# Layer 0's FFN: modulation sums by VectorE in pieces loaded ahead, a second F-tile in plain products, and other places for the way out's first operands

## The chip, the cores and the metric

The kernel runs on one core of a Trainium2 chip. TensorE (PE) multiplies matrices, VectorE (DVE), ScalarE (ACT) and GpSimd (POOL) work on tiles element by element, and SyncE (SP) issues nearly all DMAs. Each engine takes its instructions in order; semaphores tie them together. The metric is device time in microseconds. The kernel before takes 1764.14 us, the median of three runs (1763.58 to 1764.52).

## The reference

Two layers over 512 latent tokens (x) and 256 context tokens (ctx) of width 1024. Each layer has an attention and an FFN, and each of these is framed by a modulation: six vectors a layer, for each of the two kinds of token, from a conditioning vector.

```python
for l in range(DEPTH):
    mx = s_c @ mod_w[l] + mod_b[l]        # latent tokens
    mc = s_cc @ mod_w[l] + mod_b[l]       # context tokens
    shx1, scx1, gx1, shx2, scx2, gx2 = split(mx, 6)
    ...
    x = x + gx1 * attention(...)
    x = x + gx2 * swiglu(rms(x, norm_ffn_w[l]) * (1 + scx2) + shx2, ffn_w_in[l], ffn_w_out[l])
    ...  # the same for ctx in layer 0; the last layer needs x alone behind its attention

def swiglu(h, w_in, w_out):
    gate, up = split(h @ w_in, 2)         # 1024 -> 2 x 2816
    return (silu(gate) * up) @ w_out      # 2816 -> 1024
```

The parts of a modulation are numbered 0 to 5 in that order: (1, 5) is the FFN gate of layer 1. A part has 1024 columns and is worked out in four chunks of 256 columns. For the latent tokens and the context tokens there are two sums over the same weights, two "streams"; where only the latent tokens need it, one.

## The kernel before

Everything is float32. A product is made of three matmuls in TensorE's faster float type: each operand is split into a high part (a cast, by ACT) and a low part (a subtraction, by DVE or POOL), and high x high, low x high and high x low are summed. `wbh` and `wbl` are the two parts of a weight block, `hT` of the normed tokens, `hTt` of the difference T2.

Layer 0's FFN has two stages. **Gate and up** goes over 22 F-tiles of 128 hidden columns. F-tile 0 is computed in plain products, from four weight quarters (G1, U1 over the first half of the 1024 inputs, G2, U2 over the second) times two halves of the tokens. Every other tile takes the seven products P1 to P7 of a Strassen-Winograd scheme: their left operands are blocks of the tokens or differences of them (B.., T1 to T4), their right ones quarters of the weights or differences of those (S1 to S4, `ws`). Each product is 12 matmuls of 128x384 (L862). ACT copies partial results out of PSUM (`s`, L867), DVE adds them up (`cg` L885, `c` L890) and forms the hidden values (`hid` L895, L896), which are stored to memory as one tile of 768 tokens (`hidm`) and read back later. `block_order` is the order of the products, written out by hand; PE follows the program's order in this stage. The weight operands are made six ahead in a ring.

**The way out** (`way_out0`) multiplies the hidden values by the second weight in two passes of three token tiles, six PSUM banks each. For each F-tile it loads `hr` (hidden values) and `wdr` (weights), splits both (ACT L924 and L339, DVE L925 and L340), and runs 18 matmuls (L960 to L962) of 128x512.

In these two stages the modulations of what comes next are worked out beside the matmuls. Four chunks of (0, 5) are multiplied by PE (`mod_steps`, L181 and L190). The others go through `mods_by_pool`: a chunk's weights are loaded in two pieces (`modw`, 512 KB), ACT multiplies four blocks by their scalars (L216), POOL adds them (L217 to L222), PE sums over the partitions (the row, L228) and turns the row into columns (L237), and DVE adds a bias (`modc`, L249). `hooks`, a table by F-tile, says when a group of chunks begins, and when its row and its columns are issued; a group in the gate and up stage takes 2.5 F-tiles. `gates_out` turns a gate's columns back into rows (`gps`, L261, and DVE's copy `grow`, L263) and keeps them in memory.

All engines but PE are ordered by a scheduler that goes by dependences and priorities; pools and rings set when a buffer is free.

Of the kernel before, what the change touches and what calls it, by code (L numbers as in the profile page):

```python
# [18 lines left out]
P = 128  # L19
# [43 lines left out]
def backbone(es: ExitStack, tc: tile.TileContext, x, c, ctx, c_ctx, mod_w, mod_b, norm_mix_w, norm_ffn_w,  # L63
# [133 lines left out]
    def mods_by_pool(chunks, pool, bank=None):  # L197

        width = 256
        def bank_tile(name, shape):  # L200
            return tr_tile(name, shape) if bank is None else p_1.tile(shape, F32, name=name, tag=bank)

        all_accs = []
        for l, part, n, streams in chunks:
            c0 = part * D + n * width
            accs = [pool.tile([P, width], F32, name="ma", tag="ma", bufs=4) for _ in range(streams)]
            for pc in range(2):
                w = pool.tile([P, 4, width], F32, name="modw", tag="mw", bufs=2)
                nc.sync.dma_start(
                    w, mod_w[l, pc * 4 * P:(pc + 1) * 4 * P, c0:c0 + width].rearrange("(j p) n -> p j n", p=P))  # L210
                for i, acc in reversed(list(enumerate(accs))):

                    pr = pool.tile([P, 4, width], F32, name="modp", tag="mp", bufs=1) if i else w
                    for k in range(4):
                        kk = 8 * i + 4 * pc + k
                        nc.scalar.activation(pr[:, k], w[:, k], AF.Copy, scale=cols[:, kk:kk + 1])  # L216
                    nc.gpsimd.tensor_add(pr[:, 0:2], pr[:, 0:2], pr[:, 2:4])  # L217
                    if pc == 0:
                        nc.gpsimd.tensor_add(acc, pr[:, 0], pr[:, 1])
                    else:  # L220
                        nc.gpsimd.tensor_add(pr[:, 0], pr[:, 0], pr[:, 1])
                        nc.gpsimd.tensor_add(acc, acc, pr[:, 0])  # L222
            all_accs.extend(accs)
        def finish():
            ps = bank_tile("modrow", [P, width])

            for j, acc in enumerate(all_accs):
                nc.tensor.matmul(ps[32 * j:32 * j + 32, :], cst[:, C_ONE:C_ONE + 32], acc, start=True, stop=True,  # L228
                                 tile_position=(0, 32 * j))
            m = len(all_accs)  # L230

            r = all_accs[0]
# [7 lines left out]
            for l, part, n, streams in chunks:  # L240
# [3 lines left out]
        return finish()  # L244
# [523 lines left out]
    def block_order(first_half, second_half, hooks=None):  # L768
# [3 lines left out]
        for f in range(2, NF):  # L772
            order += [(f, "P1"), (f, "P5"), (f - 1, "P4")] + (hooks or {}).get(f - 0.5, []) + [(f, p) for p in (("P6", "P2", "P3", "P7") if f < NF - 1 else ("P6", "P2", "P7", "P3"))]
            order += (hooks or {}).get(f, [])
        return order + [(NF - 1, "P4")]

# [11 lines left out]
    def gate_up_blocks(l, N, H, order, first_raw, next_raw, ring, ahead, early, tmp, deep, hid, singles, z, after, done=None):  # L788
# [10 lines left out]
        loaded = 0  # L799

# [28 lines left out]
        def operand(n):  # L829
# [7 lines left out]
            if n:  # L837
                f, name = need[n - 1]
                hi, lo = ops[need[n - 1]]
                (nc.gpsimd if name == "G2" else nc.vector).tensor_sub(lo, raw[need[n - 1]], f32(hi))  # L840
                if name == "U2":
                    load(f + 2)
# [7 lines left out]
        def product(f, p):  # L850
# [14 lines left out]
            def copied(tag):  # L865
                c = tmps[f, tag] = tmp.tile([P, N], F32, name=tag, tag=tag, bufs=deep)
                nc.scalar.copy(c, ps)  # L867
# [23 lines left out]
            elif p == "P4":  # L891
                if N <= 256:
                    nc.vector.tensor_mul(hid(f), gates(), bank(f, 0)[:, :2 * N])
                else:
                    nc.vector.tensor_mul(hid(f)[:, :N], gates()[:, :N], ps)  # L895
                    nc.vector.tensor_mul(hid(f)[:, N:], gates()[:, N:], tmps[f, "c2"])  # L896
# [3 lines left out]
            elif p[:2] == "U2":  # L900
                nc.vector.tensor_mul(hid(f)[:, th * N:(th + 1) * N], tmps[f, "sg"], ps)
# [314 lines left out]
    def differences():  # L1216
        t1 = wide.rearrange("p (k c) -> p k c", c=half)
        (h11, l11), (b12, b22) = (f32(z) for z in H["B11"]), rh
        with tc.high_priority(300):
            for _ in norms[NT - 1]:  # L1220
                pass
# [313 lines left out]
```

## Time and profile before

| | before |
|---|---|
| runs, median (lowest to highest) | 1764.14 us (1763.58 to 1764.52) |
| profiled execution | 1765.05 us |
| its span | 1763.3 us |
| mean granted TensorE clock | 0.983 |
| gate and up of layer 0 | 431.5 to 791.8 us |
| way out of layer 0 | 791.8 to about 987 us |
| DMA over the span | 194.67 MB, mean 110 GB/s |

The span is the profiled program from its first to its last instruction; the device time around it is 1.75 us longer. A row of a timeline has the start, the length, the engine and the line, what was written from what, and in brackets how long the engine sat idle before it and what released it. Matmul rows overlap: from start to start is what one costs.

### The profile page before, as it was taken

The numbers are of one execution on the slowest core, as the hardware profiler recorded it, in microseconds if no ns is written. First come the engines' busy times: TensorE is split into PE (matmuls) and PEld (weight loads), VectorE is DVE, ScalarE is ACT, GpSimd is POOL, SyncE is SP. The second block draws the span as 40 slices with busy tenths as digits, with TensorE's granted clock in tenths as the row PEclk, the third lists the DMA queues.
The fourth block names the chain that finished last, engine by engine and source line by source line (L and its number), as shares of the span: only waits on it lengthen the run. The fifth ranks groups of instructions, "written<-read, shape, count | busy, mean of one in ns | idle before, by whom it ended". The sixth has DMA issues, their size and how long they took to land. (4 is left out here: it accounts for less than half of the span.)

```text
span 1763.3 us, 28606 instructions
## 1 busy us (share of the span) xinstructions
PE 1671.1 (95%) x10410; PEld 1481.1 (84%) x10410; DVE 1087.6 (62%) x1848; ACT 980.9 (56%) x2123; POOL 784.1 (44%) x928
## 2 busy tenths in 40 slices
PE   6999999999899999899899989999998989999999
PEld 4887777677899999897688889899986889999887
DVE  4775555434856665665565547667666498887533
ACT  5555555554447676666554546666665555555321
POOL 2774654733216676645510366666654332222000
PEclk9999999999999999999999999999999989999999
DMA  9111322402345444558665412111104233332432
GB/s 322 43 53 60 105 89 72 144 24 60 117 153 162 147 146 149 175 162 282 203 189 171 144 37 61 37 37 41 44 22 132 66 89 103 109 102 61 132 96 72
DMA packets 214799, 194.67 MB, mean 110 GB/s; under 512 B 19648, under 2 KB 196608, under 8 KB 214656
## 3 DMA queue, kind: packets, MB, share of 16 engines
q1 hardware_dynamic: 214304, 192.62, 35.3%
q8 instruction: 82, 1.34, 0.3%
q14 instruction: 61, 0.50, 0.1%
q10 hardware_dynamic: 352, 0.21, 0.0%
HBM read 179.91 MB, written 12.87 MB: 109 GB/s over the span
## 5 line engine op out<-in xcount | busy, mean ns | idle before, releaser
L835 ACT CAST wbh<-wr 128x512 fp32r<-128x512 f32 x171 | 105.3, 619 | 91.0 <-PE p L862 57.4
L862 PE MATMUL p<-hT,wbh 128*128 128x256 f32 (+1 forms) x696 | 145.7, 303 | 0.0
L840 POOL TENSOR_TENSOR wbl<-wr,wbh 128x512 fp32r<-128x512 f32 x43 | 58.2, 1353 | 189.8 <-ACT wbh L835 175.4
L840 DVE TENSOR_TENSOR wbl<-wr,wbh 128x512 fp32r<-128x512 f32 x128 | 115.3, 905 | 43.1 <-ACT wbh L835 39.5
L435 PE MATMUL inps<-wih,hT 128*128 128x384 f32 x384 | 133.3, 347 | 3.9 <-ACT qkv L642 3.1
L437 PE MATMUL inps<-wih,hT 128*128 128x384 f32 x384 | 131.1, 341 | 0.0
L436 PE MATMUL inps<-wil,hT 128*128 128x384 f32 x384 | 129.9, 338 | 0.0
L862 PE MATMUL p<-t,wbh 128*128 128x384 f32 (+1 forms) x504 | 118.4, 321 | 3.1 <-ACT s L867 3.0
L216 ACT ACTIVATE modw<-modw,cols 128x256 f32<-128x256 f32 x192 | 83.6, 499 | 64.8 <-DMA modw<-in_mod_w_dram 64.7
L862 PE MATMUL p<-hTt,wbh 128*128 128x256 f32 (+1 forms) x504 | 109.0, 308 | 9.4 <-DVE hTt L925 6.1
L862 PEld LDWEIGHTS p<-hT,wbh 128*128 128x128 f32 x696 | 114.4, 194 | 3.0 <-issue 2.5
L835 ACT CAST wbh<-ws 128x512 fp32r<-128x512 f32 x126 | 73.3, 582 | 63.2 <-PE p L862 39.1
L862 PE MATMUL p<-hT,wbl 128*128 128x256 f32 (+1 forms) x348 | 104.8, 301 | 1.9 <-DVE wbl L840 1.9
L340 POOL TENSOR_TENSOR wil<-wir,wih 128x768 fp32r<-128x768 f32 x42 | 79.2, 1888 | 61.2 <-ACT wih L339 60.4
L960 PE MATMUL dps<-wdh,hdh 128*128 128x512 f32 x252 | 101.5, 403 | 4.5 <-ACT hdh L924 3.1
L961 PE MATMUL dps<-wdl,hdh 128*128 128x512 f32 x252 | 100.8, 400 | 3.2 <-DVE wdl L340 3.2
L217 POOL TENSOR_TENSOR modw<-modw 128x512 f32<-128x512 f32 x48 | 65.6, 1367 | 80.1 <-ACT modw L216 75.5
L962 PE MATMUL dps<-wdh,hdl 128*128 128x512 f32 x252 | 100.4, 398 | 0.0
L340 DVE TENSOR_TENSOR wdl<-wdr,wdh 128x1024 fp32r<-128x1024 f32 x62 | 82.5, 1333 | 22.4 <-ACT wdh L339 22.1
L565 POOL TENSOR_SCALAR Pt<-Pt,rc 128x256 f32<-128x256 f32 (+3 forms) x96 | 69.0, 730 | 58.5 <-DVE rc L562 49.9
L862 PEld LDWEIGHTS p<-hTt,wbh 128*128 128x128 f32 x504 | 84.4, 195 | 12.0 <-DVE hTt L925 6.6
L862 PE MATMUL p<-b,wbh 128*128 128x384 f32 x360 | 92.8, 339 | 0.4 <-ACT s L867 0.4
(321 smaller groups left out, 5268.5 us busy)
## 6 DMA issues: line engine op xcount, KB each, us to landing
modw<-in_mod_w_dram SPq DMA_DIRECT2D x96, 512.0 KB, 4.7
wr<-in_ffn_w_in_dram SPq DMA_DIRECT2D x176, 256.0 KB, 3.0
wdr<-in_ffn_w_out_dram SPq DMA_DIRECT2D x66, 512.0 KB, 3.5
wir<-in_od_w_in_dram SPq DMA_DIRECT2D x96, 128.0 KB, 2.3
hidm<-hid SPq DMA_DIRECT2D x22, 384.0 KB, 2.5
hr<-hidm SPq DMA_DIRECT2D x22, 192.0 KB, 2.7
x<-in_x_dram SPq DMA_DIRECT2D x8, 512.0 KB, 3.6
wir<-in_ev_w_in_dram SPq DMA_DIRECT2D x16, 256.0 KB, 2.7
```

The costliest lines, as they stand in the source:

```text
L216: nc.scalar.activation(pr[:, k], w[:, k], AF.Copy, scale=cols[:, kk:kk + 1])
L340: (sub or nc.vector).tensor_sub(lo, raw, f32(hi))
L435: nc.tensor.matmul(ps, hs[0][:, k, :], a, start=k == 0, stop=False)
L436: nc.tensor.matmul(ps, hs[0][:, k, :], b, start=False, stop=False)
L437: nc.tensor.matmul(ps, hs[1][:, k, :], a, start=False, stop=k == KT - 1)
L565: nc.gpsimd.tensor_scalar(p[:, :n], p[:, :n], rc[:, hh:hh + 1], 1.0, ALU.mult, ALU.mult)
L835: nc.scalar.copy(hi, w)
L840: (nc.gpsimd if name == "G2" else nc.vector).tensor_sub(lo, raw[need[n - 1]], f32(hi))
L862: nc.tensor.matmul(ps, w[:, k, :], H[b][h][:, k, :], start=first and k == 0 and q == 0, stop=final and k == 3 and q == 2, skip_group_check ...
L960: nc.tensor.matmul(ps, hh, a, start=f == 0, stop=False)
L961: nc.tensor.matmul(ps, hh, b, start=False, stop=False)
L962: nc.tensor.matmul(ps, hl, a, start=False, stop=f == NF - 1)
```

## The change

It does seven things.

1. *Modulations.* `mod_steps` is no longer used in this stage. `mod_stream` is a generator called twice in every F-tile from the third on: each call can issue one load (three buffers, two pieces ahead), one piece's products, one group's row, or the columns of the row before. Of a two-stream piece, the first stream's products and sums are DVE's (one multiplication and seven multiply-adds per chunk of 128x256), the second's are ACT's and POOL's as before; of one-stream chunks every other goes to DVE. ACT's products are issued behind the last PSUM copy.
2. *Groups.* Six groups of two chunks with two streams ((0, 5), (1, 0), (1, 1)) and one of four chunks with one stream (1, 2) are in the gate and up stage, three groups of four chunks ((1, 3), (1, 4), (1, 5)) in the way out. Gates follow one to a call.
3. *F-tile 1* is computed in plain products, with F-tile 0's; the first token half of both, then the second. The products of the two tiles stand between the last normed tokens and the differences. There are 156 products of 12 matmuls instead of 155.
4. *The first operands* (G1, U1) lie in columns of `hT` that are written later, not in a tile of their own.
5. *Hidden values* are staged and stored in halves of the tokens, in two buffers.
6. *The way out's first pass* uses a ring of four places for split operands: weights in the rows of `hT`, hidden values in those of T2, raw hidden values in the rest of T2's rows. The first two banks of a pass are others than those of the last products.
7. Pools of layer 1 open earlier.

```diff
-    def mods_by_pool(chunks, pool, bank=None):
+    def mod_stream(groups, pool, bank):
         width = 256
+        pieces = [(g, c, pc) for g in groups for c in g for pc in range(2)]
+        accs, raws, full, rows = {}, [], [], []
...
+        def load(g, c, pc):
+            l, part, n, streams = c
+            w = pool.tile([P, 4, width], F32, name="modw", tag="mw", bufs=3)
+            nc.sync.dma_start(w, mod_w[l, pc * 4 * P:(pc + 1) * 4 * P, part * D + n * width:
+                                       part * D + (n + 1) * width].rearrange("(j p) n -> p j n", p=P))
+            raws.append((g, c, pc, w))
+        def products(g, c, pc, w):
...
+            for i, acc in enumerate(accs[c]):
+                scale = [cols[:, 8 * i + 4 * pc + k:8 * i + 4 * pc + k + 1] for k in range(4)]
+                if i == 0 and (streams == 2 or c[2] % 2 == 0):
                     for k in range(4):
+                        if pc or k:
+                            nc.vector.scalar_tensor_tensor(acc, w[:, k], scale[k], acc, ALU.mult, ALU.add)
+                        else:
+                            nc.vector.tensor_scalar(acc, w[:, k], scale[k], None, ALU.mult)
+                    continue
...
+        while pieces or raws or full or rows:
+            if rows:
+                for _ in rows.pop():
+                    pass
+            if full:
+                rows.append(sums(full.pop()))
+                next(rows[0])
+            if len(raws) == 2 or not pieces and raws:
+                with behind("evac"):
+                    products(*raws.pop(0))
+            if pieces:
+                load(*pieces.pop(0))
+            yield
...
+    def block_rest(f0, hook=None, done=(1,)):
+        order = []
+        step = [hook] if hook else []
+        for f in range(f0, NF):
+            order += [(f, "P1"), (f, "P5")] + [(f - 1, "P4")] * (f - 1 in done or f > f0) + step
+            order += [(f, p) for p in (("P6", "P2", "P3", "P7") if f < NF - 1 else ("P6", "P2", "P7", "P3"))] + step
         return order + [(NF - 1, "P4")]
+
+    def block_order0(last_norm, differences, last_difference, hook):
+        order = []
+        for th, after in (("1", (last_norm, differences)), ("2", (None, last_difference))):
+            for f in range(2):
+                order += [(f, w + th) for w in QUARTERS] + [after[f]] * bool(after[f])
+        return order + block_rest(2, hook, ())
...
-                    nc.vector.tensor_mul(hid(f)[:, :N], gates()[:, :N], ps)
-                    nc.vector.tensor_mul(hid(f)[:, N:], gates()[:, N:], tmps[f, "c2"])
+                    for a, c in enumerate((ps, tmps[f, "c2"])):
+                        nc.vector.tensor_mul(hid(f, a), gates()[:, a * N:(a + 1) * N], c)
+                        done(f, a)
...
-            banks = [singles.pool.tile([P, 512], F32, name="dps", tag=tag, bufs=2) for tag in ("p0", "p0", "p1", "p1")]
-            banks += [p_1.tile([P, 512], F32, name="dps", tag=tag) for tag in (("tr0", "tr1"), ("acc0", "acc1"))[p]]
+            banks = [p_1.tile([P, 512], F32, name="dps", tag=tag) for tag in (("tr0", "tr1"), ("acc0", "acc1"))[p]]
+            banks += [singles.pool.tile([P, 512], F32, name="dps", tag=tag, bufs=2) for tag in ("p1", "p1", "p0", "p0")]
...
+                raw = pool.tile([P, 3, P], F32, name="hr", tag="hr", bufs=3) if p else raws[f % len(raws)]
...
+                    w, h = places[f % len(places)]
+                split_into(w, wr.rearrange("p (k c) -> p k c", k=4))
                 split_into(h, raw)
...
+    parts = [(0, 5), (1, 0), (1, 1)]
+    groups = [[(l, part, n + a, 2) for a in range(2)] for l, part in parts for n in (0, 2)]
+    groups.append([(1, 2, n, 1) for n in range(4)])
...
+        rows = [[z[0][:, 2 * a:2 * a + 2, :].rearrange("p a (b c) -> p (a b) c", c=256) for z in hT] for a in range(4)]
+        places = [(rows[a], [z[:, a].rearrange("p (t c) -> p t c", c=P) for z in t2]) for a in range(4)]
...
+        def mod_hook1(p, f):
+            turn["pass"] = p
+            if (f % 5 < 4 if p == 0 else f > 7) and next(streams[1], True):
+                gate_hook(1, None)
```

How the instructions stand on the engines, in three places. First VectorE in one F-tile in the middle of the gate and up stage, before:

```order
L826 TENSOR_TENSOR ws<-ws,wr 128x512
L840 TENSOR_TENSOR wbl<-ws,wbh 128x512
L840 TENSOR_TENSOR wbl<-wr,wbh 128x512
L885 TENSOR_TENSOR cg<-pz,s_5578 128x384
L826 TENSOR_TENSOR ws<-wr,ws 128x512
L840 TENSOR_TENSOR wbl<-ws,wbh 128x512
L885 TENSOR_TENSOR cg<-p_5584,s_5637 128x384
L890 TENSOR_TENSOR c_5704<-p_5565,s_5597 128x384
```

The same stretch of an F-tile of the changed kernel, where `ma` is the running sum of a modulation chunk and `cols` holds the scalars:

```order
L867 TENSOR_TENSOR ws<-ws,wr 128x512
L886 TENSOR_TENSOR wbl<-ws,wbh 128x512
L225 TENSOR_SCALAR ma<-modw,cols 128x256
L886 TENSOR_TENSOR wbl<-wr,wbh 128x512
L223 SCALAR_TENSOR_TENSOR ma<-modw,cols,ma 128x256 x2
L931 TENSOR_TENSOR cg<-pz,s_5566 128x384
L223 SCALAR_TENSOR_TENSOR ma<-modw,cols,ma 128x256
L867 TENSOR_TENSOR ws<-wr,ws 128x512
L886 TENSOR_TENSOR wbl<-ws,wbh 128x512
L223 SCALAR_TENSOR_TENSOR ma<-modw,cols,ma 128x256
L931 TENSOR_TENSOR cg<-p_5572,s_5642 128x384
L223 SCALAR_TENSOR_TENSOR ma<-modw,cols,ma 128x256 x2
```

Modulation products now stand between the weights' low parts and the sums of the PSUM banks. Second ScalarE in the same stage, before:

```order
L216 ACTIVATE modw<-modw,cols 128x256 x2
L835 CAST wbh<-ws 128x512
L216 ACTIVATE modw<-modw,cols 128x256 x2
L835 CAST wbh<-wr 128x512
L867 COPY s_6126<-p_6113 128x384
L835 CAST wbh<-wr 128x512
L867 COPY s_6145<-p_6132 128x384
L216 ACTIVATE modp<-modw,cols 128x256 x4
L835 CAST wbh<-ws 128x512
L216 ACTIVATE modw<-modw,cols 128x256 x4
```

And in the changed kernel:

```order
L876 CAST wbh<-wr 128x512
L913 COPY s_5566<-p_5553 128x384
L876 CAST wbh<-wr 128x512
L913 COPY s_5585<-p_5572 128x384
L229 ACTIVATE modp<-modw,cols 128x256 x4
L876 CAST wbh<-ws 128x512
L876 CAST wbh<-wr 128x512
L913 COPY s_5642<-p_5553 128x384
L229 ACTIVATE modp<-modw,cols 128x256 x4
L876 CAST wbh<-ws 128x512
```

The products that ACT keeps now stand directly behind a copy `s`, four at a time, and those of the other stream are gone from it. Third VectorE at the end of layer 1's gate and up stage, in the changed kernel:

```order
L936 TENSOR_TENSOR p_18403<-p_18403,s_18431 128x256
L931 TENSOR_TENSOR cg<-p_18418,s_18459 128x256
L939 TENSOR_TENSOR hid<-cg,p_18403 128x512
L289 COPY grow<-gps 8x128
L366 TENSOR_TENSOR wdl<-wdr,wdh 128x1024
```

The copy of a gate's row, `grow`, stands there behind the last hidden values; before, it stood in layer 0's way out. On TensorE its transpose (`gps`) stands directly ahead of the first sum of layer 1's way out.

More of the change, by code (lines that the diff above doesn't have):

```diff
@@ new lines, in bank_tile @@
+            one = bank()
+            return tr_tile(name, shape) if one is None else p_1.tile(shape, F32, name=name, tag=one)
+        def load(g, c, pc):
[4 more added lines that the diff above has]
+            raws.append((g, c, pc, w))
@@ L836, in operand, with low @@
                 ops[need[n]] = hi, lo
[L837 to L842, printed above, removed]
+            low(n - 1)
+        def low(n):
+            if n < 0 or n in lows:
+                return
+            lows.add(n)
+            f, name = need[n]
+            hi, lo = ops[need[n]]
+            (nc.gpsimd if name == "G2" else nc.vector).tensor_sub(lo, raw[need[n]], f32(hi))
+            if name == "U2":
+                load(f + 2)
         def bank(f, i):
@@ L919, in gate_up_blocks @@
                     n += 1
+                elif n == len(early) + ahead:
+                    low(n - 1)
             i += 1
@@ L953, in ready_hid @@
+                turn["load"] = nc.sync.dma_start(wr, ffn_w_out[0, f * P:(f + 1) * P, :])
+                if p:
+                    w = [pool.tile([P, 4, 256], F32R, name=name, tag=name, bufs=3) for name in ("wdh", "wdl")]
+                    h = [pool.tile([P, 3, P], F32R, name=name, tag=name, bufs=3) for name in ("hdh", "hdl")]
+                else:
+                    w, h = places[f % len(places)]
+                split_into(w, wr.rearrange("p (k c) -> p k c", k=4))
                 split_into(h, raw)
@@ L1214, in backbone, with last_norm @@
     mods0 = []
+    def last_norm():
+        with tc.high_priority(300):
+            for _ in norms[NT - 1]:
+                pass
     def differences():
@@ L1241, in backbone, with hid_stage, hid_store @@
     stage = {}
[L1243 to L1249 removed]
+    def hid_stage(f, th):
+        stage[f, th] = tmp.pool.tile([P, half], F32, name="hid", tag="hid", bufs=2)
+        return stage[f, th]
+    def hid_store(f, th):
+        nc.sync.dma_start(hidm[f][:, th * half:(th + 1) * half], stage.pop((f, th)))
@@ L1251, in one_z @@
     def one_z(name):
         return acc_tile(name, one=0)
-    waiting = []
-    def mod_by_pe(n):
-        def call():
-            pool = mods0[0].pool
-            waiting.append(mod_steps(0, 5, n, lambda shape, name: pool.tile(shape, F32, name=name, tag="mw", bufs=2), pool,
-                                     "acc1", room=("ma", 4)))
-            next(waiting[-1])
-        return call
-    def mod_start(chunks, pool, bank):
-        return lambda: waiting.append(mods_by_pool(chunks, pool().pool, bank))
@@ L1267, in mod_rows, with mod_hook @@
-    def mod_rows():
-        next(waiting[0])
-    def mod_cols():
-        for _ in waiting.pop(0):
-            pass
-    def gates_out(*gates, bank="acc1"):
-        def call():
-            for l, part, i in gates:
-                gate_mem(l, part, i, bank)
-        return call
+    parts = [(0, 5), (1, 0), (1, 1)]
+    groups = [[(l, part, n + a, 2) for a in range(2)] for l, part in parts for n in (0, 2)]
+    groups.append([(1, 2, n, 1) for n in range(4)])
+    streams = {}
+    def mod_hook():
+        if not streams:
+            streams[0] = mod_stream(groups, mods0[0].pool, lambda: "acc1")
+        if next(streams[0], True):
+            gate_hook(0)
```

139 lines of the change are left out of this document (54 added, 85 removed).

## The prediction

> **What bounds the kernel now.** I read the busy shares, PE's waits by releaser between 432 and 980 us (layer 0's FFN: gate and up products to 792, then the way out), the windows of its stages, and the timeline at each wait.
>
> ```profile
> PE 1671.1 (95%) x10410; PEld 1481.1 (84%) x10410; DVE 1087.6 (62%) x1848; ACT 980.9 (56%) x2123; POOL 784.1 (44%) x928
> ...
> PE p L862 <- ACT s L867: 5.7, 4, 3.0
> PE dps L961 <- DVE wdl L340: 3.2, 2, 1.6
> PE dps L960 <- ACT hdh L924: 3.1, 1, 3.1
> PE p L862 <- DVE hTt L925: 3.1, 1, 3.1
> PE dps L960 <- ACT wdh L339: 1.4, 2, 1.0
> PE p L862 <- DVE wbl L840: 1.1, 1, 1.1
> PE dps L960 <- DVE hid L895: 0.8, 1, 0.8
> ```
>
> PE (TensorE) is busy for 95% of the span. So only three things count: work taken off PE or put on it, its waits, and the slow stretches behind waits. These waits, with the .90 and 1.49 in the next rows, sum to 20.8 us. Those rows are matmuls of 128x384: the first on `b`, and the first on T2 (`hTt`).
>
> ```profile
> 447.80 0.97 PE L862 MATMUL p<-b,first 128*128 128x384 f32 x4 [1.49 <-DVE b L324]
> ...
> 457.76 0.51 PE L862 MATMUL p<-t,wbh 128*128 128x384 f32 x2
> 458.11 0.34 PE L862 MATMUL p<-t,wbl 128*128 128x384 f32 x1
> 459.35 0.44 PE L862 MATMUL p<-hTt,wbh 128*128 128x384 f32 x1 [0.90 <-ACT hTt L924]
> 462.84 0.69 PE L862 MATMUL p<-hTt,wbh 128*128 128x384 f32 x1 [3.05 <-DVE hTt L925]
> ```
>
> Two matmuls start between 457.76 and 458.11: .174 us each when nothing disturbs. The windows of the stages say what a wait costs in all (columns: length; busy time and count of PE, PEld, DVE, ACT, POOL; granted PE clock; DMA share; GB/s):
>
> ```profile
> 455.00:471.00 16.00, 12.05 (x52) 11.47 (x51) 14.71 (x15) 5.80 (x10) 1.65 (x2) 0.79 0.37 119
> ...
> 582.00:619.00 37.00, 37.00 (x220) 36.34 (x219) 23.61 (x36) 27.53 (x61) 29.64 (x26) 1.00 0.47 143
> 710.00:741.00 31.00, 26.57 (x133) 25.61 (x132) 21.35 (x27) 19.88 (x44) 20.04 (x18) 0.89 0.63 196
> 792.00:838.00 46.00, 42.06 (x173) 33.81 (x173) 26.66 (x26) 27.97 (x54) 25.68 (x21) 0.93 0.87 282
> 838.00:880.00 42.00, 38.96 (x167) 30.12 (x165) 23.07 (x24) 23.44 (x47) 21.97 (x18) 0.96 0.64 207
> 880.00:933.00 53.00, 50.86 (x233) 41.48 (x233) 36.08 (x53) 29.64 (x47) 7.93 (x10) 0.97 0.61 186
> ```
>
> From 455 to 471 PE ran 52 matmuls, 9.0 us of work in 16: **7.0 us** lost, near twice the waits of 3.95, and the granted clock is .79. Where the clock is half, a mean of .89 over 31 us (710 to 741) is 6.8 us at half rate, 3.4 lost beside the waits. The Trainium skill ("TensorE: Matmul & The Clock Gate", Part 1) puts the slow clock behind an idle window of about 3.4 us. The row of 455 disagrees in part: its longest wait was 3.05.
>
> Why ACT is late stands in its own rows: modulation copies (L216) wait for their weights' DMA, and casts and copies that PE needs stand behind them.
>
> ```profile
> L216 ACT ACTIVATE modw<-modw,cols 128x256 f32<-128x256 f32 x192 | 83.6, 499 | 64.8 <-DMA modw<-in_mod_w_dram 64.7
> 851.48 1.71 ACT L216 ACTIVATE modw<-modw,cols 128x256 f32<-128x256 f32 x4 [8.12 <-DMA modw<-in_mod_w_dram]
> ```
>
> **The change, part by part.** Negative is time saved.
>
> *Modulations on PE.* Four chunks go from PE to the vector engines; a seventh group of sums comes to the gate-up stage.
>
> ```profile
> 502.15 0.50 PE L190 MATMUL modcol<-cst,modr 128*128 128x2 f32 x4
> 503.04 1.07 PE L181 MATMUL mod<-modw,s_pad 128*32 128x256 f32 x16 [0.38 <-DVE modc L249]
> 504.04 0.62 PE L862 MATMUL p<-hT,wbh 128*128 128x384 f32 x2
> ...
> 582.85 0.64 PE L228 MATMUL modrow<-ma,cst 128*32 128x256 f32 x8
> 583.42 0.61 PE L862 MATMUL p<-hT,wbh 128*128 128x384 f32 x2
> ...
> 589.79 0.50 PE L237 MATMUL modcol<-cst,ma 128*128 128x4 f32 x4
> 590.15 0.60 PE L862 MATMUL p<-hTt,wbh 128*128 128x384 f32 x2
> ```
>
> Columns and next chunk take 502.15 to 504.04, 1.9 us, and .1 in the pair behind. Three such, the first chunk without columns (1.1) and the last columns (.5): **-7.6**. A group's row costs .67+.1 and its columns .36+.1: **+1.2** for the seventh here, and **+1.2** in the way out, which gets three groups for two.
>
> *F-tile 1 in plain products.* 156 products stand for 155; one is 12 matmuls of .174: **+2.1**. T2 is first read behind 18 products, 37.5 us, and a transpose of about 1, so near 470 us; it was there by 462.8. The wait goes: **-7.0**. The first `b` operand is read after 16 products, near 465; it was there at 447.8: **-1.7** (.2 of restart with the 1.5). The wait for DVE's `wbl` near 434 goes (**-1.3**). In its place comes the second gate quarter's low half, which is POOL's:
>
> ```profile
> 434.05 1.75 POOL L840 TENSOR_TENSOR wbl<-wr,wbh 128x512 fp32r<-128x512 f32 x1
> ```
>
> It ended at 435.8, queued behind a subtraction for `b` that waits for the out-projection's last rows. Sixteen plain matmuls for three now stand ahead of these rows, so they end 13 x .174 = 2.3 us later, less a PE wait of .5 that the first ones fill: POOL is done near 437.6. PE has only 8 more matmuls and the quarter's first two ahead of it, so wants it near 435. Between nothing (POOL's queue turns out faster) and 6 (3 us and as much again, by the ratio of the T2 place) I take **+3**, the wait alone.
>
> *ACT's waits for `s`.* A piece's products now stand behind the last PSUM copy, and weights are loaded two pieces ahead in three buffers. ACT also loses the products that DVE takes. The 5.7 us of waits, the 3.4 of slow clock and about 1 of restarts go: **-10.1**. On SP a `modw` load waits for the products three pieces back, and queued behind it are the `wr` loads and the half stores. `wbh` and `wbl` run up to six products, 12 us of PE, ahead, which covers a wait like the 8.12 above; without that cover the waits for `s` return as waits for `wbl`.
>
> *DVE takes products.* In F-tiles 3 to 14 each tile gets one TENSOR_SCALAR and seven SCALAR_TENSOR_TENSOR of 128x256. That shape isn't in the trace; its neighbours are:
>
> ```profile
> L697 DVE SCALAR_TENSOR_TENSOR e<-e,rt 128x768 f32<-128x768 f32 x32 | 40.8, 1275 | 1.1
> L719 DVE SCALAR_TENSOR_TENSOR o<-o,rs_o,subln 128x128 f32<-128x128 f32 x32 | 15.0, 470 | 6.0 <-POOL rs_o L159 5.6
> ...
> L1094 DVE TENSOR_SCALAR xT<-xT,aff,modc 128x256 f32<-128x256 f32 x8 | 3.2, 407 | 0.1
> ...
> L840 DVE TENSOR_TENSOR wbl<-wr,wbh 128x512 fp32r<-128x512 f32 x65 | 65.8, 1020 | 35.7 <-ACT wbh L835 35.6
> L840 DVE TENSOR_TENSOR wbl<-ws,wbh 128x512 fp32r<-128x512 f32 x63 | 42.9, 681 | 2.8 <-ACT wbh L835 2.8
> ```
>
> On the line between 470 (128) and 1275 ns (768), 256 elements take .63. Before, a tile of 14.7 us (seven products and its share of the rows) has DVE busy for 23.61 x 14.7/37 = 9.4. After: 9.4 + .4 + 7 x .63 = 14.2 of a PE tile of 7 x 2.08 plus a row and columns, 15.2. It fits, narrowly. From below nothing; from above, each product at 1.2 us gives 18.2, 3 too much in each of 12 tiles, +36. I take **+4**, one stall with its slow clock, by the row 582 to 619: DVE and POOL together have 53 us of work in 37 there, and PE doesn't idle. POOL gets less to do: the code gives it 2 pieces a tile instead of 3.2.
>
> The same subtraction takes 1020 ns in one place and 681 in another. The Trainium skill ("SBUF — State Buffer", Who interferes with whom) says that a DVE instruction with two SBUF inputs and a GpSimd one that reads SBUF block each other fully. The spread of the two rows agrees. Strictly taken it makes the slower rival, below.
>
> *Way out.* Behind the wait of 3.1 for `hdh`, at 804:
>
> ```profile
> 805.12 0.63 PE L961 MATMUL dps<-wdl,hdh 128*128 128x512 f32 x1
> 805.55 0.63 PE L962 MATMUL dps<-wdh,hdl 128*128 128x512 f32 x1
> ```
>
> The third F-tile's operands came late, and 13 matmuls at .43 follow; the same shape takes .23 in the rows of 1639 below. With four tiles in `hT` and T2 before the stage begins (72 matmuls, 16.4 us of PE), the 3.1, 2.6 and .3 go: **-6.0**. Of the two later places each loses its waits (.95+1.58; .48+1.60) and slow clock (.04 x 42 = 1.7; .03 x 53 = 1.6) and .4: **-4.6 and -4.1**; the ring is four deep and ACT no longer stands before unlanded weights. Starting on other banks than the ones that `hid` reads: **-1.1**.
>
> Against it: all 24 `modw` loads of the last three parts now stand on SP ahead of the first pass's last operands: 12.6 MB, and 18 times .72 MB of operands and 1.2 MB of the next pass, 26.8 MB. PE would need them within 82 us (20 tiles of 18 matmuls at .23): 327 GB/s. The row 792 to 838 moved 282 at a share of .87, so 324 at a full share. From nothing (it just fits, some being loaded before) over 13 (95 us at 282) to 47 (129 us at the 207 of the next row, whose share of .64 leaves room). I take **+7**, half of the middle, since the first four tiles are in place and the last loads serve sums that can slip.
>
> *Gates.* Single gates save two waits on DVE that lie below the list's last row, together 1.2. One, layer 1's FFN gate, is left for layer 1's way out, where the first sum's bank then waits for DVE:
>
> ```profile
> 1639.11 0.40 PE L1005 MATMUL dps<-hT,hTt 128*128 128x512 f32 x1
> 1639.34 0.40 PE L1006 MATMUL dps<-hT,hTt 128*128 128x512 f32 x1
> ...
> 1639.38 0.69 DVE L893 TENSOR_TENSOR hid<-cg,p 128x512 f32<-128x512 f32 x1 [1.22 <-PE p L862]
> ...
> L263 DVE COPY grow<-gps 8x128 f32<-8x128 f32 x4 | 1.1, 274 | 0.4 <-PE gps L261 0.4
> ```
>
> The gate's copy (.27) stands behind that `hid`, so the sums start near 1640.3 for 1639.1: +1.2. Together **0**.
>
> **Sum.** Gate-up: -7.6 +1.2 +2.1 -7.0 -1.7 -1.3 +3 -10.1 = -21.4, and +4. Way out: -6.0 -4.6 -4.1 -1.1 +1.2 = -14.6, and +7. Total -25.0 from the profiled 1765.05 (span 1763.3): 1740.0. The median of the runs stands .9 lower: **1739**.
>
> **Rivals.**
> - *DVE and POOL exclude each other, slower than before.* In F-tiles 3 to 14 the two-input DVE work of a tile is nine 128x512 instructions (six `wbl`, three `ws`) at .68, 6.1 us, and seven products of at least .47, 3.5 with some length for the double width. POOL has 29.64 x 14.7/37 = 11.8 a tile now, and between 7.4 (scaled by its pieces) and 11.8 then; at 8.5 the two take 18.1 of 15.2, 2.9 too much, 35 in 12 tiles for the +4: **1770**. It decides from 2.4 too much a tile on. For it: 1.02 against .68 for `wbl`. Against it: the same sum was 6.1 + 11.8 = 17.9 in 14.7 before, and PE didn't idle. Chance .09. The Trainium skill's rule above, read strictly, would have made that earlier stretch 3 us a tile longer; the trace shows no such loss.
> - *DMA holds the first pass* at 250 GB/s: 107 us for 82, +25 for the +7: **1757**. For it: the share of .87 already; chance .12.
> - *The change doesn't do what it says*: waits for `s` and operands come back behind the new loads on SP. PE's own saving (-6), T2 and `b` (-9) less the plain product and POOL's low half (+5) leave about -10: **1754**. Chance .12.
> - *Forecast*: 1728 (both allowances nothing) to 1750: .67.
>
> **Range and chances.** 1727 to 1757 takes in the forecast with 1 us to spare below, the DMA rival's 1757 and the fourth case's 1754, and leaves the slower rival and what is worse than these three out: .17. About .2% (3.5 us) is what a measurement can tell from no change: faster .85 (of the DMA rival and the fourth case, a part comes out higher than their price), within .07, slower .08.
>
> **What would show it.** Right: no L181 row between 432 and 792; no wait for `hTt` or `b`; PE's waits for `s` under 1 us; DVE at 14 of 15 us in F-tiles 3 to 14; no wait over 1 us in the way out's first 16 us; a wait of 1.2 us at layer 1's first sum. Wrong: PE waits for `wbl` in every tile from 3 to 14 (DVE or the port), DMA share near 1 with waits for `wdh` in the first pass, or a wait well over 3 us for POOL's `wbl` at the start.

## The result, and the profile after

The changed kernel takes 1734.36 us (median of four runs, 1730.21 to 1735.18), the kernel before 1764.33 in the same comparison: a ratio of 0.9826, with a 95% interval of 0.9809 to 0.9843. That is 30 us less; the forecast was 1739, 25 less. The profile read below is of the longest of the four runs, 1735.18.

PE's waits in the FFN of layer 0 of the changed kernel, from the view of waits between 432 and 960 us (in total, times, longest):

```profile
PE p L908 <- POOL wbl L886: 1.8, 1, 1.8
PE dps L1005 <- DVE x L469: 1.3, 1, 1.3
PE p L908 <- DVE c L936: 1.1, 1, 1.1
```

All the waits that the prediction lists are gone: `s`, `hTt`, `b`, `wdl`, `hdh` and the others. One of the three that stand instead was forecast: the second gate quarter's low half, made by POOL. Its rows on PE:

```profile
437.39 0.52 PE L908 MATMUL p<-hT,wbh 128*128 128x384 f32 x2
439.70 0.45 PE L908 MATMUL p<-hT,wbl 128*128 128x384 f32 x1 [1.79 <-POOL wbl L886]
...
441.50 0.53 PE L908 MATMUL p<-hT,wbl 128*128 128x384 f32 x1
441.82 0.84 PE L908 MATMUL p<-hT,wbh 128*128 128x384 f32 x2
...
444.67 0.52 PE L908 MATMUL p<-hT,wbh 128*128 128x384 f32 x2
445.03 0.34 PE L908 MATMUL p<-hT,wbl 128*128 128x384 f32 x1
```

The matmuls run at half rate again, .32 each from 441.50, and .18 from 444.67 on. Two windows of the changed kernel (columns as in the prediction), one in the middle of gate and up, one at the start of the way out:

```profile
520.00:550.00 30.00, 30.00 (x176) 29.75 (x180) 27.53 (x47) 17.95 (x39) 17.49 (x14) 1.00 0.56 167
774.00:820.00 46.00, 46.00 (x205) 38.17 (x205) 36.09 (x53) 25.68 (x47) 13.82 (x13) 1.00 0.98 337
```

In the first VectorE is busy for 27.53 of 30 us, in the second the DMA engines for .98 of the time at 337 GB/s. In both PE has no idle time and the whole clock. Both resources that the prediction feared are nearly full, and PE waits for neither here.

Where the 29.9 us between the two spans lie, by the first and last rows of each stage on PE (the last matmul of the way out before starts at 993.87; the 987 of the table of before is too early):

| stage | before | after | difference | forecast |
|---|---|---|---|---|
| up to the out-projection of layer 0 | 326.33 | 329.68 | +3.35 | 0 |
| out-projection, gate and up | 465.51 | 444.66 | -20.85 | -21.4 and +4 |
| way out, first to last matmul | 202.03 | 187.89 | -14.14 | -14.6 and +7 |
| from there to layer 1's way out | 645.24 | 646.71 | +1.47 | 0 (the gate's +1.2 less 1.2 saved earlier) |
| the rest | 124.2 | 124.5 | +0.3 | 0 |

The first row isn't the change's to explain: in the profiles of the changed kernel and its twelve variants that stretch takes between 325.8 and 329.7 us, though the edits of the variants all lie behind it. The mean granted clock in it was .97 for .99 before.

### The profile page after: what moved, and what is told of

Read it like the earlier page. It is cut to its first block, busy times and chain, and to the rows that moved or that the text cites. A ratio compares the mean times of both kernels' runs of the same rounds, so it can differ in the third digit from the quotient of the medians.

```text
span 1733.4 us, 28526 instructions
## 1 busy us (share of the span) xinstructions
PE 1664.7 (96%) x10366; PEld 1482.3 (86%) x10366; DVE 1148.4 (66%) x1999; ACT 943.0 (54%) x2020; POOL 719.0 (41%) x867
## 4 chain that ended last, share of the span: by engine, by line
PE 38%; DVE 7%; DMA 4%; ACT 2%; POOL 2%; issue 2%; SPq 0%; ACTq 0%; POOLq 0%; DVEq 0%
PE p L908 11%; PE inps L461 3%; PE inps L462 3%; PE inps L463 3%; PE dps L1051 2%; PE dps L1053 2%; PE dps L1052 2%; DMA wdr<-in_ffn_w_out_dram 2%; PE pz L908 2%; PE av L738 2%; PE dps L1005 1%; PE dps L1006 1%; PE dps L1007 1%; PE ops L785 1%; PE ops L786 1%
## 5 line engine op out<-in xcount | busy, mean ns | idle before, releaser
L908 PE MATMUL p<-hT,wbh 128*128 128x256 f32 (+1 forms) x712 | 149.7, 303 | 0.0
L886 DVE TENSOR_TENSOR wbl<-wr,wbh 128x512 fp32r<-128x512 f32 x127 | 108.5, 862 | 17.6 <-ACT wbh L876 13.1
L908 PE MATMUL p<-t,wbh 128*128 128x384 f32 (+1 forms) x488 | 112.8, 317 | 0.0
L230 POOL TENSOR_TENSOR modp<-modp 128x512 f32<-128x512 f32 x40 | 57.4, 1436 | 119.3 <-ACT modp L229 119.3
L862 POOL TENSOR_TENSOR wr<-wr 128x512 f32<-128x512 f32 x41 | 62.2, 1518 | 101.8 <-DVE ws L867 95.2
L223 DVE SCALAR_TENSOR_TENSOR ma<-modw,cols,ma 128x256 f32<-128x256 f32 x140 | 89.8, 642 | 2.4 <-DMA modw<-in_mod_w_dram 0.2
L886 DVE TENSOR_TENSOR wbl<-ws,wbh 128x512 fp32r<-128x512 f32 x123 | 83.5, 680 | 1.7 <-ACT wbh L876 1.6
L908 PEld LDWEIGHTS p<-t,wbh 128*128 128x128 f32 x488 | 84.2, 189 | 0.0
L581 ACT ACTIVATE Pt<-sc,nm 128x256 f32<-128x256 f32 (+3 forms) x96 | 67.8, 710 | 28.9 <-DVE nm L577 14.9
```

The lines of the kernel that those rows point to most:

```text
L223: nc.vector.scalar_tensor_tensor(acc, w[:, k], scale[k], acc, ALU.mult, ALU.add)
L581: turn["exp"] = nc.scalar.activation(p[:, :n], s, AF.Exp, bias=nm[:, c1], accum_out=sm[:, c1])
L862: nc.gpsimd.tensor_sub(w, raw[f, "G1"], w)
L908: nc.tensor.matmul(ps, w[:, k, :], H[b][h][:, k, :], start=first and k == 0 and q == 0, stop=final and k == 3 and q == 2, skip_group_check ...
```

## The experiments

Each is the changed kernel with one edit, unless it says otherwise. The kernel before ran beside them each time. Stage lengths below are from profiles: "gate and up" is from the out-projection's first matmul to the way out's first (444.66 in the changed kernel), "way out" from its first to its last matmul (187.89).

### What took the waits for the copies `s` away

The prediction took 10.1 us for these waits and gave three reasons for their going: weights are loaded ahead, the products stand behind the last PSUM copy, and VectorE takes a part. Five runs try them.

**Everything by ACT and POOL.**

```diff
-                if i == 0 and (streams == 2 or c[2] % 2 == 0):
+                if False:
```

> The changed kernel, but every modulation product by ACT and every sum by POOL again; loads still run two pieces ahead. Theory 'weights ahead' (the waits for s went because ACT no longer stands before weights that haven't landed): PE's waits for s stay near nothing, ACT is at 14 of 15 us a tile in F-tiles 3 to 14 (10.6 and eight more copies of .43), POOL at 13; time 1734 to 1745. Rival 'VectorE's share is what did it': ACT or POOL exceed the tile, waits for s or wbh in most tiles, some 1 us a tile in 12 tiles and more, 1748 to 1765.

Measured: 1803.93 us, ratio 1.0227 (1.021 to 1.0244), slower than before; neither theory's range. Gate and up takes 507.9 us. PE's waits, and two windows:

```profile
PE modrow L244 <- POOL ma L233: 42.8, 12, 5.3
...
PE p L908 <- ACT s L913: 0.8, 1, 0.8
...
550.00:580.00 30.00, 22.64 (x116) 20.22 (x115) 12.50 (x19) 17.35 (x39) 17.26 (x17) 0.83 0.34 106
580.00:610.00 30.00, 23.15 (x120) 21.12 (x119) 13.91 (x20) 17.67 (x40) 19.87 (x19) 0.89 0.42 131
```

The waits for `s` are .8 us, but PE, whose order is fixed, waits for late sums at the group's row. ACT and POOL are busy for 17 to 20 of 30 us: neither is full, they take turns. There is one product buffer (`modp`), which ACT fills and POOL empties. So this run says nothing on whether the two could carry the work, and a second was made.

**The same, with the first stream's products written over the weights**, as in the kernel before. The edit stands on top of the one above.

```diff
-            for i, acc in enumerate(accs[c]):
+            for i, acc in reversed(list(enumerate(accs[c]))):
...
-                pr = pool.tile([P, 4, width], F32, name="modp", tag="mp", bufs=1)
+                pr = pool.tile([P, 4, width], F32, name="modp", tag="mp", bufs=1) if i else w
```

> As act_sums (all products by ACT, all sums by POOL, loads two pieces ahead), but the first stream's products are written over the loaded weights, as in the kernel before, so that ACT needn't wait until POOL has read the one product buffer. In act_sums ACT and POOL were each busy for only 18 of 30 us while rows waited 42.8 us for POOL's sums. Theory 'one product buffer': the two engines no longer take turns; rows wait for POOL under 10 us, 1735 to 1755. Rival 'ACT and POOL can't carry it at this pace': POOL is busy for 26 of 30 us and more, rows still wait 20 us and more, 1770 to 1800.

Measured: 1743.91 us, ratio 0.99 (0.9878 to 0.9921). Gate and up takes 447.06 us, 2.4 more than the changed kernel. Two of PE's waits:

```profile
PE dps L1005 <- DVE x L469: 4.6, 1, 4.6
...
PE modrow L244 <- POOL ma L233: 1.0, 4, 0.4
```

The theory of the one product buffer held: the rows wait 1.0 us for POOL, where they waited 42.8, and no wait for `s` is left. So VectorE's share isn't what saves the time in gate and up. In the whole kernel it is worth 9.6 us, most of it in the way out (193.59, +5.7), where one bank waits 4.6 us for a residual sum. Why that sum is late there was not tried.

**Products right behind their own load.**

```diff
-            if len(raws) == 2 or not pieces and raws:
-                with behind("evac"):
-                    products(*raws.pop(0))
             if pieces:
                 load(*pieces.pop(0))
+            if raws:
+                with behind("evac"):
+                    products(*raws.pop(0))
             yield
```

> The changed kernel, but a piece's products are issued right behind its own load instead of two pieces later. Theory 'weights ahead': ACT and DVE again stand before weights that are still on their way (5.5 us from issue to landing), waits for s or wbl come back, 5 to 15 us: 1739 to 1750, and idle time before modp and ma with the DMA as releaser. Rival 'the products' place behind the PSUM copies and VectorE's share are enough': within 2 us of the changed kernel.

Measured: 1730.84 us, ratio 0.9819 (0.9798 to 0.9839). The theory of the prediction fell: without loads ahead nothing is lost that the runs can tell. In gate and up PE waits 2.8 us for `c` in three times, and for `s` not at all. ACT and VectorE stood idle for modulation weights for 1.0 us in all, for 3.8 in the changed kernel: behind the copy, the weights have landed even without a lead.

**Neither loads ahead nor the place behind the copy**, and **loads ahead without the place**. The same lines are changed in the run above and in the changed kernel.

```diff
-                with behind("evac"):
-                    products(*raws.pop(0))
+                products(*raws.pop(0))
```

> The changed kernel, with products right behind their own load and without the rule that ACT's come behind the last PSUM copy; what is left of the change to the modulations is VectorE's share, the even pace (two calls a tile) and the third buffer. Theory 'place behind the copy' (it alone took PE's waits for s away): waits for s of 3 us and more come back with slow clock, 1737 to 1750. Rival 'VectorE's share and the even pace': no waits for s over 1 us in sum, within 3 us of the run no_ahead.

> The changed kernel, loads two pieces ahead, but without the rule that ACT's and DVE's products come behind the last PSUM copy. It is the fourth of four: with both 1734, behind the copy alone (no_ahead) 1731, with neither 1750 and waits for c of 15.4 us. Theory 'weights landed': either one gives a load time to land, so loads ahead alone do it too: waits for c and s under 3 us in sum, gate and up within 3 us of the changed kernel, 1731 to 1737. Rival 'place': the products' place is what counts, and without it DVE's eight products stand in front of the sums that PE waits for: waits for c of 8 us and more, 1743 to 1752.

Measured: 1749.63 us without both, ratio 0.993 (0.9912 to 0.9949), and 1751.61 without the place alone, 0.9937 (0.9914 to 0.996). The place decides the time: without it gate and up takes 468.6 and 463.1 us, 24 and 18 more than the changed kernel, whether weights are loaded ahead or not. But it isn't ACT that is late. PE's waits, first without both, then with loads ahead and without the place:

```profile
PE p L907 <- DVE c L935: 15.4, 9, 3.4
PE p L907 <- ACT s L912: 2.6, 3, 1.5
```

```profile
PE p L907 <- DVE c L935: 12.7, 9, 3.4
...
PE p L907 <- ACT s L912: 0.4, 1, 0.4
```

And VectorE's timeline at one of the nine, with the matmul pair that waited:

```profile
568.35 2.32 DVE L223 SCALAR_TENSOR_TENSOR ma<-modw,cols,ma 128x256 f32<-128x256 f32 x2
570.59 0.54 DVE L930 TENSOR_TENSOR cg<-p,s 128x384 f32<-128x384 f32 x1
571.06 0.93 DVE L223 SCALAR_TENSOR_TENSOR ma<-modw,cols,ma 128x256 f32<-128x256 f32 x2
571.90 0.55 DVE L935 TENSOR_TENSOR c<-p,s 128x384 f32<-128x384 f32 x1
...
572.51 0.62 PE L907 MATMUL p<-b,wbh 128*128 128x384 f32 x2 [0.91 <-DVE c L935]
```

Four modulation products stand in front of the two sums that free PE's banks, and one pair of them takes 2.32 us. VectorE is nearly full, so what stands in front of a sum decides. From 550 to 580 it is busy for 26.7 of 30 us here, and for 27.0 in the changed kernel, where PE waits for `c` once, 1.1 us. The edit takes the place from ACT's products and from VectorE's; which of the two counts was not tried apart. The run with loads ahead lies in both ranges of its rival (12.7 us of waits for the "8 and more", 1751.61 for "1743 to 1752").

So these runs say what the three reasons are worth in time, and leave open which of them ended the waits for `s`. With any one of the three taken away, PE waits .8 us for `s` at the most, for 5.7 in the kernel before. Without the place and the loads ahead together 2.6 us come back.

### What VectorE can carry

```diff
-                if i == 0 and (streams == 2 or c[2] % 2 == 0):
+                if g[0][1] in (5, 0, 1) and streams == 2 or i == 0 and c[2] % 2 == 0:
```

> The changed kernel, but both streams' products are DVE's in F-tiles 3 to 14 (two TENSOR_SCALAR and fourteen SCALAR_TENSOR_TENSOR a tile); POOL then has only its weight work there. If .64 us an instruction holds, DVE's tile is 9.4 + .8 + 14 x .64 = 19 of PE's 15.2: PE waits for wbl in every one of those tiles, near +3.8 x 12 = 45, 1770 to 1785. If POOL's adds were what stretched DVE (the port theory), DVE runs at its undisturbed lengths, .49 an instruction and .68 a low half, 8.9 + .8 + 6.9 = 16.6: +10 to +20, 1745 to 1755.

Measured: 1748.14 us, ratio 0.9917 (0.9895 to 0.994). Gate and up takes 459.65 us, 15 more; PE waits 10.8 us for `c` in seven times. It is the range of the port theory (POOL's adds stretch VectorE's instructions), not that of a fixed length. VectorE's groups between 470 and 700 us, first in the changed kernel, then in this one:

```profile
L223 DVE SCALAR_TENSOR_TENSOR ma<-modw,cols,ma 128x256 f32<-128x256 f32 x98 | 62.7, 640 | 1.4 <-DMA modw<-in_mod_w_dram 0.2
L886 DVE TENSOR_TENSOR wbl<-wr,wbh 128x512 fp32r<-128x512 f32 x45 | 42.8, 968 | 5.9 <-ACT wbh L876 5.2
L886 DVE TENSOR_TENSOR wbl<-ws,wbh 128x512 fp32r<-128x512 f32 x47 | 31.9, 679 | 0.9 <-ACT wbh L876 0.9
```

```profile
L223 DVE SCALAR_TENSOR_TENSOR ma<-modw,cols,ma 128x256 f32<-128x256 f32 x175 | 90.4, 548 | 0.0
L886 DVE TENSOR_TENSOR wbl<-wr,wbh 128x512 fp32r<-128x512 f32 x44 | 31.7, 725 | 1.0 <-ACT wbh L876 1.0
```

With POOL's adds gone, and ACT's products with them, the same instructions take 548 for 640 ns, and 725 for 968. The changed kernel's own trace tells the two apart: of the 98 instructions of the first row, the 40 with no POOL instruction beside them took .47 to .49 us each, 37 of these with ACT at work. The 58 beside POOL took .47 to 1.57, and .75 on average. The Trainium skill ("SBUF — State Buffer", Who interferes with whom) has a VectorE instruction with two inputs in SBUF contend with a POOL instruction that reads SBUF. These rows go that way. The third row does not: its 47 instructions took .67 to .69 us, and 26 of them ran beside POOL.

### F-tile 1

F-tile 1 through P1 to P7 again, in the order of before.

```diff
-        for th, after in (("1", (last_norm, differences)), ("2", (None, last_difference))):
-            for f in range(2):
-                order += [(f, w + th) for w in QUARTERS] + [after[f]] * bool(after[f])
-        return order + block_rest(2, hook, ())
+        order = [(0, w + "1") for w in QUARTERS] + [last_norm, differences, (1, "P1"), (1, "P2")]
+        order += [(0, w + "2") for w in QUARTERS] + [last_difference] + [(1, p) for p in ("P5", "P6", "P3", "P7")]
+        return order + block_rest(2, hook)
```

> The changed kernel, but F-tile 1 goes through P1 to P7 again, in the order that the kernel before had. By the prediction's steps T2's wait with its slow clock (7.0) and that of b (1.7) come back and one product (2.1) goes: +6.6 on the changed kernel, near 1741, PE waiting for hTt at the start. Rival 'DVE and POOL, freed of other work at the start, make T2 in time': -2, near 1732, no wait for hTt.

Measured: 1736.11 us, ratio 0.9839 (0.9824 to 0.9854), 1.8 above the changed kernel's median. PE's waits in the stage:

```profile
PE p L906 <- DVE b L350: 3.0, 1, 3.0
PE p L906 <- DVE hTt L972: 2.4, 1, 2.4
...
PE p L906 <- POOL wbl L884: 1.8, 1, 1.8
PE p L906 <- DVE b L972: 1.6, 1, 1.6
```

The waits for T2 and `b` are back, and gate and up takes 451.74 us, +7.1 for the +6.6 forecast. The total shows less, since the stretch ahead of it took 326.4 for 329.7 us in this profile. The step is borne out in its stage; the total can't tell it apart.

### The way out's ring, and its banks

**Only two F-tiles in the rows of `hT` and T2.** The others use the ring of three in new memory.

```diff
-                raw = pool.tile([P, 3, P], F32, name="hr", tag="hr", bufs=3) if p else raws[f % len(raws)]
+                early = not p and f < 2
+                raw = raws[f] if early else pool.tile([P, 3, P], F32, name="hr", tag="hr", bufs=3)
...
-                if p:
+                if not early:
```

> The changed kernel, but only the first two F-tiles of the way out's first pass lie in the rows of hT and T2; the others go through the ring of three in memory that comes free at the end of gate and up, as before. Theory 'late memory': the wait for the third tile's operands comes back, 3 us and its slow clock, +6 on the changed kernel, near 1740; later waits of 1 to 3 us for wdl or wdh are possible beside the faster modulation loads. Rival 'ACT's place did it' (the cast was late since ACT stood before unlanded modulation weights): no wait over 1 us there, within 2 us of the changed kernel.

Measured: 1741.8 us, ratio 0.987 (0.9855 to 0.9884), +7.4. The way out takes 195.66 (+7.8). The matmul and the cast that it waits for:

```profile
782.62 0.79 PE L1006 MATMUL dps<-wdh,hdh 128*128 128x512 f32 x1 [4.40 <-ACT hdh L973]
...
782.06 0.51 ACT L973 CAST hdh<-hr 128x384 fp32r<-128x384 f32 x1 [10.66 <-DMA hr<-hidm]
```

ACT was idle for 10.66 us for the load of hidden values itself: the theory of late memory held, and the rival that ACT stood before modulation weights fell.

**Other banks last.** In both passes p1, p1, p0, p0 first, the single banks last.

```diff
-            banks = [p_1.tile([P, 512], F32, name="dps", tag=tag) for tag in (("tr0", "tr1"), ("acc0", "acc1"))[p]]
-            banks += [singles.pool.tile([P, 512], F32, name="dps", tag=tag, bufs=2) for tag in ("p1", "p1", "p0", "p0")]
+            banks = [singles.pool.tile([P, 512], F32, name="dps", tag=tag, bufs=2) for tag in ("p1", "p1", "p0", "p0")]
+            banks += [p_1.tile([P, 512], F32, name="dps", tag=tag) for tag in (("tr0", "tr1"), ("acc0", "acc1"))[p]]
```

The reason to try it is a wait that the prediction didn't have: in the changed kernel PE stops at the boundary to layer 1, where before it ran through. First the kernel before, then the changed kernel:

```profile
993.87 0.39 PE L962 MATMUL dps<-wdh,hdl 128*128 128x512 f32 x1
994.10 0.28 PE L435 MATMUL inps<-wih,hTc 128*128 128x256 f32 x1
```

```profile
962.23 0.39 PE L1007 MATMUL dps<-wdh,hdl 128*128 128x512 f32 x1
964.81 1.09 PE L339 MATMUL npt<-cst,nh 128*128 128x128 f32 x8 [2.19 <-ACT nh L334]
967.86 0.58 PE L461 MATMUL inps<-wih,hTc 128*128 128x256 f32 x1 [1.96 <-DVE x L469]
```

> The changed kernel, but in both passes of the way out the banks go p1, p1, p0, p0, then the single ones: the last sums of the stage lie in banks that layer 1's first matmuls don't take. Theory 'the bank order moved the wait': the 2.2 and 2.0 us in which PE waits at the layer's boundary (for nh, then for x) shrink to under 1 in all, with the slow clock behind them, -4 to -6, 1729 to 1730; the first pass starts on p1 without a wait. Rival 'DVE is late at the boundary anyway' (the residual sums stand behind weights' low halves): PE still waits 3 us and more there, within 2 us of the changed kernel.

Measured: 1741.33 us, ratio 0.9877 (0.9854 to 0.9901), slower than the changed kernel by 7. At the boundary:

```profile
958.93 0.39 PE L1007 MATMUL dps<-wdh,hdl 128*128 128x512 f32 x1
960.45 0.36 PE L461 MATMUL inps<-wih,hTc 128*128 128x256 f32 x1 [1.13 <-DVE x L469]
```

The gap fell from 5.6 to 1.5 us, as the theory had it: the bank order moved that wait. But the gain was given back and more: from the last matmul of the way out to the out-projection of layer 1 it takes 348.7 us for 340.9. Longer waits for `wil`, `lex` and `e` stand in layer 1's attention. In that stage the scheduler's order changes with each edit; which of the changes costs the 8 us was not tried.

### Two small waits

**The low half by VectorE.**

```diff
-            (nc.gpsimd if name == "G2" else nc.vector).tensor_sub(lo, raw[need[n]], f32(hi))
+            (nc.gpsimd if name == "G2" and (f or not done) else nc.vector).tensor_sub(lo, raw[need[n]], f32(hi))
```

> The changed kernel, but the low half of F-tile 0's second gate quarter is DVE's instead of POOL's. In the changed kernel PE waits 1.79 us for POOL there and then runs matmuls at half rate for some 3.5 us, 4 in all. If POOL's queue is the cause, the wait goes and the time falls by 3 to 4, near 1731. Rival: DVE's queue is as late at that place (it has the last tokens' norm), a wait of 1 to 2 us for DVE stands there instead, no gain.

Measured: 1736.77 us, ratio 0.9846 (0.9818 to 0.9873). The rival held: PE waits 1.9 us for DVE there.

**One more call of the hook in the second pass.**

```diff
-            if (f % 5 < 4 if p == 0 else f > 7) and next(streams[1], True):
+            if (f % 5 < 4 if p == 0 else f > 6) and next(streams[1], True):
```

> The changed kernel, but the way out's hook is called once more in the second pass, so that layer 1's FFN gate is turned into rows there and not in layer 1's way out. The wait of .9 us for its copy at layer 1's first sum goes, and a transpose of .35 comes to layer 0's way out: -1, inside what the runs can tell; the row of the wait shows it. Rival: something else is late at that place by then (hid's store or the bank), and a wait of like size stays.

Measured: 1733.33 us, ratio 0.9831 (0.9813 to 0.985), not to be told from the changed kernel. The changed kernel's wait at layer 1's first sum, which is gone here:

```profile
1607.74 0.27 PE L287 MATMUL gps<-cst,modc 128*8 128x128 f32 x1
1608.94 0.50 PE L1051 MATMUL dps<-hT,hTt 128*128 128x512 f32 x1 [0.93 <-DVE grow L289]
```

**Both: that call, and a place of its own for the second gate quarter**, so that it is split ahead of the last tokens' norm.

```diff
+    first = rawh.pool.tile([P, 2, 4, P], F32R, name="first")
...
-        early = [[z[0][:, 4 * a:4 * a + 4, half:] for z in hT] for a in range(2)]
+        early = [[z[0][:, 4 * a:4 * a + 4, half:] for z in hT] for a in range(2)] + [[first[:, 0], first[:, 1]]]
```

> The changed kernel with two edits: the second gate quarter of F-tile 0 has a place of its own, so that its cast and POOL's low half are issued ahead of the last tokens' norm, and the way out's hook is called once more (as in gate_13). By the trace of the changed kernel the first takes the wait of 1.79 us and some 2.4 of slow clock away, the second the wait of .9 at layer 1's first sum: -4 to -5, 1729 to 1730, and neither wait shows. Rival: the gain is taken back behind it, where the next operand's cast is late or the layer's boundary waits longer: 1732 to 1735.

Measured: 1735.44 us (five runs, 1731.59 to 1738.64), ratio 0.9841 (0.9823 to 0.986). The wait for POOL is gone, and PE stops at the next thing:

```profile
438.10 0.34 PE L908 MATMUL p<-hT,wbl 128*128 128x384 f32 x1
442.50 1.97 PE L339 MATMUL npt<-cst,nhs 128*128 128x128 f32 x8 [4.06 <-ACT nhs L334]
444.12 0.67 PE L908 MATMUL p<-hT,wbh 128*128 128x384 f32 x1
```

The last tokens' norm follows the out-projection's end, and its transpose stands behind F-tile 0's first products. No run beats the changed kernel by more than the runs differ among themselves.

## Why the prediction was right, step by step

- **PE's own work** (-7.6, +1.2, +2.1). No L181 row stands in the stage any more. Before, L181 and L190 took 5.9 us of PE from start to start, and 1.1 of waits for `modc` went with them. A group's row costs .57 in the lines shown (582.85 to 583.42), where the prediction has .67, so each +1.2 is .1 too high.
- **T2 and `b`** (-7.0, -1.7, less 2.1 for the product). The waits are gone, and undoing the step costs 7.1 us in its stage for the 6.6 forecast.
- **POOL's low half** (+3). The mechanism held. The 23 matmuls from 437.39 to 445.03 took 7.6 us for 4.0 at .174: 3.6 lost for the 3, by a wait of 1.79 and the ten matmuls at .32 behind it. Whether the clock falls behind this wait is in part chance, as the last section shows. Two runs show that a cure at this place only uncovers the next late thing.
- **The waits for `s`** (-10.1). They are gone; the reasons given were wrong in part. None of the three is needed alone for that: without any one of them PE waits .8 us for `s` at the most. For the time, loads ahead count for nothing that shows (1730.84 us without), and VectorE's share for little in gate and up (447.06 us without it, for 444.66). The place of the products behind the last PSUM copy counts: without it 1749.63 and 1751.61 us. And what it protects in the changed kernel is VectorE's sums `c`, no longer ACT's copies.
- **VectorE's tile** (+4). An instruction of 128x256 takes 640 ns for the .63 estimated. That is luck: with no POOL instruction beside it, it takes .47 to .49, and the mean comes from some that POOL stretches. VectorE is busy for 27.5 of 30 us, and the only wait of the stage for it is 1.1 us near 771. The allowance was too much by some 3 us.
- **The way out** (-6.0, -4.6, -4.1, -1.1, +1.2). 187.89 us for 202.03, with one new wait of 1.3 between the passes. The ring's part was shown by undoing it: +7.8.
- **The DMA of the first pass** (+7). The share went to .98, and nobody waited: the loads just fit, the lower bound of that term. This is the term that was mis-sized most.
- **The gate** (+1.2 in layer 1). Measured 0.93 of wait and 1.2 from the transpose to the first sum.
- **Not forecast:** 5.6 us at the boundary to layer 1 for .2 before; another order of the banks takes it down to 1.5. Up to layer 1's out-projection the loss is made good (340.9 us for 343.1). From there to its way out it takes 305.8 us for 302.1: PE's waits sum to 13.7 us in both, and the mean granted clock was .97 for .98.
- **The total** is closer than its terms. Without the two allowances, +4 and +7, the forecasts of the two stages are -21.4 and -14.6, and -20.9 and -14.1 were measured. The allowances came to almost nothing. But 5 us were lost outside these stages (3.35, 1.47 and .3 in the table), so 30 us less came out and not 35.

The rival of VectorE and POOL excluding each other did not decide here: single instructions are stretched, but VectorE's work still fits the tile, and the changed kernel is below that rival's time. The run with all two-stream products on VectorE went past VectorE's tile, and still stayed below the time before.

## What to carry to other kernels

When work is put on an engine that is nearly full, say for each piece behind which instruction it may stand: without the place behind the last copy out of PSUM the same work made the kernel 17 us longer with loads ahead (1751.61 for 1734.36) and 19 without (1749.63 for 1730.84). A resource at .98 is no loss as long as what it brings is wanted later than it arrives; count the bytes against the time by which they are needed. A wait taken away in front of a stage is worth little when the next input of that stage is as late: here three waits moved to the next late thing.

## What was not expected of the hardware

A single wait of 1.79 us was followed by half rate: the matmuls stay at their full rate up to 441.03, go at .32 each from 441.50 to about 444.4, and are back at .18 from 444.67 on. The wait of 1.09 us that ends at 772.16 had no such stretch behind it. The Trainium skill ("TensorE: Matmul & The Clock Gate", Part 1) tells of a slow clock after an idle window of some 3.4 us; here a wait of little over half of that was enough.

Why it came some 1.5 us late can be seen in three windows of 3.41 us (the granted clock stands behind the five engines):

```profile
437.81:441.22 3.41, 1.62 (x10) 1.52 (x10) 3.36 (x5) 2.42 (x5) 2.59 (x4) 1.00 1.05 288
441.22:444.63 3.41, 3.41 (x12) 3.41 (x11) 1.01 (x2) 3.25 (x5) 2.50 (x2) 0.50 0.97 282
444.63:448.05 3.42, 3.42 (x24) 3.39 (x24) 2.32 (x6) 2.08 (x6) 0.00 (x0) 1.00 1.03 286
```

In all fourteen profiles the granted clock is 1 or .5, and the times at which it changes lie whole multiples of 3.41 us apart. The wait lies inside the stretch that ends at 441.22, in which PE was busy for 1.62 of 3.41 us, and the clock is half in the next one. The same wait for this operand's low half, 1.79 to 1.86 us, stands in twelve of the profiles. In eight of them the next stretch is at half clock. In four it isn't, and in three of these four the wait lies across the end of a stretch (with other banks last, from 436.13 to 437.92 across 436.46). So whether a wait of this size also costs the clock depends on when it falls, and a microsecond or two between two profiles can be that.
